# Sixteen more activations kept in SBUF, list making spread over more blocks, and sums paced to the end of a fused transformer layer

## Chip, cores and metric

One core of one Trainium2 chip runs the whole layer as one program. The metric is the device time of one execution in microseconds (us).

## What is computed

One decoder layer over 512 positions of width 1024: attention of two kinds, a norm, and then a retrieval feed-forward (PEER) with 16384 experts, a second norm. The change lies in the feed-forward:

```python
q = (hx @ w_pq).reshape(PEER_CHUNK, PEER_HEADS, 2, PEER_HALF)
sc = jnp.einsum('thpd,hpnd->thpn', q, sub_keys).astype(jnp.float32)
v_half, i_half = lax.top_k(sc, PEER_TOPK)
...
top_s, top_pos = lax.top_k(cand, PEER_TOPK)
idx = jnp.take_along_axis(cand_idx, top_pos, axis=-1)
g = jax.nn.softmax(top_s, axis=-1)
a = jax.nn.gelu(jnp.einsum('thkd,td->thk', u_tab[idx], hx), approximate=False)
return jnp.einsum('thk,thkd->td', (g * a).astype(hx.dtype), v_tab[idx])
```

Each position picks 128 experts (8 heads of 16), takes the dot of its row with each expert's row of `u_tab`, applies gelu, weighs with the gate `g`, and sums the experts' rows of `v_tab`.

## The kernel before

The 512 positions are four tiles of 128. They are served in two ways.

**Dense way**, for the second half of tile 1 and for tiles 2 and 3 (320 positions, `TU`): all 16384 experts are multiplied, in 128 blocks of 128 experts. The first loop ("U blocks", U0 to U127, lines 826 to 836) loads a block of `u_tab` (`raw`, SP queue), splits it into a rounded part `hi` (ScalarE, line 86) and the rest `lo` (VectorE, line 87), and `u_block` (line 802) multiplies it with the normed input `h2h`, `h2l` by 24 matmuls of 320 columns into `st`; ScalarE applies gelu (line 812). The result of U0 to U31 (`a_r`) stays in SBUF; that of U32 to U127 (`a_s`, `NS` = 96) is written to DRAM (`a_d`, line 817, ScalarE's DMA queue) and read again later (`a_b`, line 871, SP queue).

The second loop ("V blocks", V0 to V127 in the order of `order`, lines 893 to 938) multiplies the activation of a block with its gate (`w`, lines 874 and 875), splits that (`wh`, `wl`), loads and splits a block of `v_tab`, and accumulates by 18 matmuls of 512 columns (`v_mm`, three tiles, two halves). The gate of eight blocks (1.5 MB) is loaded at a time by `g_load` (line 851, ScalarE's DMA queue) into `gl`, one group ahead, from `g_d` in DRAM. The last six V blocks (`LAST`) are multiplied at the end, tile by tile and half by half, each half followed by its norm (`finish`).

**Sparse way**, for tile 0 and the first half of tile 1: the chosen rows are fetched by indirect DMA on GpSimd's queue (`fetch`, line 741, 128 rows of 4 KB each, five buffers `gb`), and VectorE takes a dot (line 746) or adds the weighted row (a "sum", line 782). The half tile needs 64 fetches of `u_tab` (its other half of the lists shares the partitions), and its result goes into the gate of tile 1; tile 0 needs 128 fetches of `u_tab` and 128 of `v_tab`.

Beside the U blocks two more things are made: the **lists** of the four tiles (`topk`, VectorE mostly, in the order 1, 2, 3, 0) and the **gate** of tiles 2, 3, 1 (`make_g`: 16 steps for each tile on VectorE, ScalarE and TensorE, 8 stores of 1 MB to `g_d`, line 699). These, the dots and the sums are Python generators whose steps yield a cost; `pull` runs steps until a budget per block is used up: 2.6 for lists until list 1 is there, 1.6 after; `GRATE` = 0.52 gate steps per block once list 2 is there; `RA` = 1.7 for the half tile's dots and `RB` = 1.9 for tile 0's (a dot costs 1.25); in the V loop 1.6 per block (a sum costs 1.2), and at V116 all that is left (`pull(gt, 1e9)`, line 917), followed by tile 0's norm. Tile 0's dots begin when the half tile is done and list 0 is there (`gather_tile`); the gate of tile 1 begins when the half tile is done. `paced` keeps each dot and sum on VectorE behind the split of the block before the last.

Within these ties a scheduler, when the program is built, gives each engine its fixed order of instructions, by program order and by its planned times. Pools share SBUF as a stack: `gl`, `a_b`, `w`, `wh`, `wl` of the V stage (`vp`) lie where the lists and the gate's tiles (`sel`, `gp`) were; `h2h` and `h2l` lie in the pool `hpool` under the tags `hh` and `hl`, which `hi4` and `lo4`, the splits of V124 to V127, take over at the end.

Of the kernel before, what the change touches and what calls it, by code (L numbers as in the profile page):

```python
# [11 lines left out]
F32 = mybir.dt.float32  # L12
# [8 lines left out]
P = 128  # L21
# [6 lines left out]
NKEY = 128  # L28
DT = NT - 1
TD = DT * P  # L30
TG = 16
NTG = TD // TG
# [3 lines left out]
LOWEST = -3.0e38  # L36
NB = 32
GB = 8
NS = 96
GRATE = 0.52  # L40
HU = 64
T0U = P + HU
TU = S - T0U
LAST = 6
GBUF = 5
RA = 1.7
RB = 1.9


@with_exitstack  # L50
def layer(ctx: ExitStack, tc: tile.TileContext, A, out, dbg=None):
# [6 lines left out]
    hpool = ctx.enter_context(tc.tile_pool(name="hpool", bufs=1))  # L58
# [12 lines left out]
    g2_d = dram.tile([1, D], F32, name="g2_d")  # L71
    a_d = [dram.tile([P, TU], F32, name=f"a_d{e}") for e in range(NS)]
    g_d = dram.tile([NTG, P, NKEY, TG], F32, name="g_d")
# [21 lines left out]
    def mm3(ps, lh, ll, rh, rl, first, last):  # L95
        nc.tensor.matmul(ps, lh, rh, start=first, stop=False)  # L96
        nc.tensor.matmul(ps, lh, rl, start=False, stop=False)  # L97
        nc.tensor.matmul(ps, ll, rh, start=False, stop=last)  # L98
# [18 lines left out]
    hh = hpool.tile([P, KB, S], F32R, name="hh", tag="hh")  # L117
# [57 lines left out]
    def drain(g, n=None):  # L175
        i = 0
        while n is None or i < n:
            try:
                next(g)
            except StopIteration:  # L180
                return False
            i += 1
        return True
# [361 lines left out]
    sel_stack = ExitStack()  # L545
# [29 lines left out]
    def u_split(e):  # L575
        return split(load_raw(A["u_T"][e], [P, KB, P]), [P, KB, P])
# [23 lines left out]
    ring = ring_stack.enter_context(tc.tile_pool(name="ring", bufs=1, side="right", reuse_waits="tile"))  # L600
# [101 lines left out]
    best = {}  # L702
    budget = [0.0]
# [4 lines left out]
    weighted = []  # L708
# [19 lines left out]
    def all_g(pool, tk):  # L728
        for t in (2, 3):
            while t not in best:  # L730
                budget[0] -= next(tk, 0.0)
            yield from make_g(t, pool)
        while not weighted:
            yield
        yield from make_g(1, pool)
# [55 lines left out]
    def pull(gen, us):  # L791
        while us > 0:
            try:
                cost = next(gen)
            except StopIteration:
                return us
            if cost is None:
                return 0.0
            us -= cost
        return us  # L800

    def u_block(e):
        hi, lo = early.pop(e) if e in early else u_split(e)
        ps = psq[0].tile([P, TU], F32, name="st", tag="st", bufs=psq[1])
        for k in range(KB):
            mm3(ps, hi[:, k, :], lo[:, k, :], h2h[:, k, T0U:], h2l[:, k, T0U:], k == 0, k == KB - 1)
        pace[0], pace_next[0] = pace_next[0], split.last
        if NB <= e < NB + NS:
            a = ring.tile([P, TU], F32, name="a_s", tag="a_s", bufs=3)
        else:  # L810
            a = ring.tile([P, TU], F32, name="a_r", tag="a_r", bufs=NB)
        nc.scalar.activation(a, ps, AF.Gelu)
        acts[e] = a

    def keep(e):
        if NB <= e < NB + NS:
            nc.scalar.dma_start(a_d[e - NB], acts[e])
            acts[e] = None

    g_stack = ExitStack()  # L820
    gp = g_stack.enter_context(tc.tile_pool(name="gp", bufs=1, reuse_waits="tile"))
    tk = all_topk(gp)
    gg = all_g(gp, tk)
    c1 = c2 = 0.0
    gt = gathers()
    for e in range(NB + NS):
        u_block(e)
        keep(e)
        budget[0] = pull(tk, budget[0] + (2.6 if 1 not in best else 1.6))
        if 2 in best:  # L830
            c1 += GRATE
            while c1 >= 1.0:
                c1 -= 1.0
                drain(gg, 1)
        if 1 in lists:
            c2 = pull(gt, c2 + (RA if not weighted else RB))
    pull(tk, 1e9)
    while not weighted:
        next(gt)
    drain(gg)  # L840
    g_stack.close()
    sel_stack.close()
    psB_stack.close()
    psq[:] = ctx.enter_context(tc.tile_pool(name="psC", bufs=1, space=bass.MemoryType.PSUM, reuse_waits="tile")), 2, 6

# [1 line left out]
    vp = v_stack.enter_context(tc.tile_pool(name="vp", bufs=1, reuse_waits="tile"))  # L847
    pacc = [[accbank() for _ in range(2)] for _ in range(DT)]
    order = list(range(NB)) + list(range(NB + NS, NKEY)) + list(range(NB, NB + NS))

    def g_load(e):
        gl = vp.tile([P, NTG, GB * TG], F32, name="gl", tag="gl", bufs=2)
        nc.scalar.dma_start(gl, g_d.rearrange("g p i t -> p g (i t)")[:, :, e * TG:(e + GB) * TG])
        return gl

# [34 lines left out]
    c2 = 0.0  # L890
    tail = [None]
    last = []
    for n in range(NKEY):
        if n % GB == 0 and n + GB < NKEY:
            gls[order[n + GB]] = g_load(order[n + GB])
        if n + NB + NS < NKEY:
            u_block(n + NB + NS)
            c2 = pull(gt, c2 + 3.6)
        else:
            c2 = pull(gt, c2 + 1.6)  # L900
        if n == NKEY - 16:
            ring_stack.close()
            fin = ctx.enter_context(tc.tile_pool(name="fin", bufs=1, side="right", reuse_waits="tile"))
            tail[0] = fin
            g2r, ln2g, ln2b = (fin.tile([P, D], F32, name=nm) for nm in ("g2r", "ln2g", "ln2b"))
            dma(g2r, g2_d[0].partition_broadcast(P))
            dma(ln2g, A["ln2_g"].partition_broadcast(P))
            dma(ln2b, A["ln2_b"].partition_broadcast(P))
            xr = [fin.tile([P, D], F32, name=f"xr{t}") for t in range(NT)]
            for t in range(NT):  # L910
                dma(xr[t], x1_d[t])
            pre = [h2n] + [fin.tile([P, D], F32, name=f"pre{t}") for t in range(DT)]
            hi4 = hpool.tile([P, 4, D], F32R, name="hi4", tag="hh")
            lo4 = hpool.tile([P, 4, D], F32R, name="lo4", tag="hl")
            tail += [hi4, lo4]
        if n == NKEY - 12:
            pull(gt, 1e9)

            def finish(t, src):
                def half(s, f):  # L920
                    nc.vector.tensor_mul(pre[t][:, s], src[f], g2r[:, s])
                    nc.vector.scalar_tensor_tensor(pre[t][:, s], xr[t][:, s], ALPHA, pre[t][:, s],
                                                   op0=OP.mult, op1=OP.add)

                normalize(vp, pre[t], half)
                for f in range(2):
                    fs = slice(f * 512, (f + 1) * 512)
                    nc.vector.tensor_mul(pre[t][:, fs], pre[t][:, fs], ln2g[:, fs])
                    nc.vector.tensor_add(pre[t][:, fs], pre[t][:, fs], ln2b[:, fs])
                    dma(out[t][:, fs], pre[t][:, fs])  # L930

            finish(0, (acc0[:, 0:512], acc0[:, 512:1024]))
        blk = v_block(n)
        if n < NKEY - LAST:
            for t in range(DT):
                v_mm(t, *blk)
        else:
            last.append(blk)
# [79 lines left out]
```

## Time and profile before

| | us |
|---|---|
| median of 3 runs | 1553.13 (1549.42 to 1555.18) |
| the profiled execution | 1551.68 |
| its span, first to last instruction | 1549.9 |

| engine | busy us | share of the span |
|---|---|---|
| TensorE (PE) | 1432.2 | 92% |
| VectorE (DVE) | 1267.8 | 82% |
| ScalarE (ACT) | 826.1 | 53% |
| GpSimd (POOL) | 466.8 | 30% |

The attention and the scores take the first 362 us, the U blocks run to 981, the V blocks to 1536.6. All times in rows are us from the start of the span; the profile names lines of the kernel above (L741 is line 741). A tile's name in a row stands left of `<-` for what is written and right of it for what is read; buffer numbers are left out. PEclk is the granted clock of TensorE as a part of 2.4 GHz. The DMA share is the mean busy share of the 16 DMA engines.

### The profile page before, as it was taken

What the parts mean: (1) busy time and instruction counts of PE and PEld (TensorE: products, weight loads), DVE (VectorE), ACT (ScalarE), POOL (GpSimd) and SP (SyncE); (2) the same over time, 40 slices, a digit from 0 to 9 for tenths busy, and PEclk for the clock granted to TensorE, in tenths of its full rate; (3) what the DMA queues carried; (4) which work ended last, traced back from release to release, by engine and by line L of the source; (5) the groups of instructions that cost most, each with busy time, mean ns of one, the idle gap of its engine ahead of it and who ended that gap; (6) DMA issues with size and microseconds to landing.
All of it is one profiled execution on the core that took longest, in us unless ns stands there. A gap on an engine that the chain in (4) does not pass through costs nothing.

```text
span 1549.9 us, 22874 instructions
## 1 busy us (share of the span) xinstructions
PE 1432.2 (92%) x7837; PEld 1254.3 (81%) x7837; DVE 1267.8 (82%) x2606; ACT 826.1 (53%) x1523; POOL 466.8 (30%) x338
## 2 busy tenths in 40 slices
PE   6999998998688899999999969999989999989996
PEld 5777776888687889999999969888868778868884
DVE  7897676999888998798879848989778788879766
ACT  2465534334357889899799834344333343334440
POOL 0000000000433334454544525545434443532000
PEclk9999998999999999999999989999989999999998
DMA  8856363222767789999999999999999999999751
GB/s 312 289 182 200 130 212 103 83 85 92 250 239 283 238 310 375 357 408 394 416 342 390 405 362 409 382 379 346 340 385 342 368 372 355 363 337 362 233 171 48
DMA packets 184855, 451.43 MB, mean 291 GB/s; under 512 B 15841, under 2 KB 90977, under 8 KB 181538
## 3 DMA queue, kind: packets, MB, share of 16 engines
q1 hardware_dynamic: 75426, 241.28, 43.0%
q0 software_dynamic: 46080, 167.79, 28.9%
q10 hardware_dynamic: 63232, 40.90, 8.7%
q8 instruction: 61, 1.00, 0.3%
q14 instruction: 56, 0.46, 0.1%
HBM read 404.00 MB, written 45.88 MB: 290 GB/s over the span
## 4 chain that ended last, share of the span: by engine, by line
PE 47%; issue 14%; DMA 13%; DVE 11%; POOL 8%; ACT 5%; POOLq 0%; SPq 0%; DVEq 0%; ACTq 0%
POOL gb L741 8%; PE acc L97 7%; PE acc L98 7%; PE acc L96 7%; DMA raw<-v_blk 5%; PE bank L96 5%; PE bank L97 4%; PE bank L98 4%; DMA gl<-g_d 3%; DMA raw<-u_T 3%; DVE lo L87 3%; PE st L96 2%; PE st L98 2%; PE st L97 2%; ACT hi L86 2%
## 5 line engine op out<-in xcount | busy, mean ns | idle before, releaser
L86 ACT CAST hi<-raw 128x1024 fp32r<-128x1024 f32 x286 | 299.8, 1050 | 333.5 <-DMA raw<-v_blk 111.4
L87 DVE TENSOR_TENSOR lo<-raw,hi 128x1024 fp32r<-128x1024 f32 x286 | 348.7, 1221 | 119.0 <-ACT hi L86 113.4
L96 PE MATMUL st<-h2h,hi 128*128 128x320 f32 x1024 | 326.3, 319 | 27.6 <-ACT hi L86 27.6
L98 PE MATMUL st<-h2h,lo 128*128 128x320 f32 x1024 | 322.0, 316 | 17.5 <-DVE lo L87 17.5
L97 PE MATMUL st<-h2l,hi 128*128 128x320 f32 x1024 | 321.7, 314 | 0.0
L96 PE MATMUL acc<-hi,wh 128*128 128x512 f32 x768 | 302.2, 394 | 17.3 <-ACT hi L86 17.0
L97 PE MATMUL acc<-lo,wh 128*128 128x512 f32 x768 | 303.8, 396 | 5.0 <-DVE lo L87 4.6
L98 PE MATMUL acc<-hi,wl 128*128 128x512 f32 x768 | 301.8, 393 | 0.0
L741 POOL DMA_INDIRECT gb<-v_tab,ei x128 | 182.4, 1425 | 240.2 <-DVE acc L782 222.3
L746 DVE SCALAR_TENSOR_TENSOR gb<-gb,h2n 128x1024 f32<-128x1024 f32 x192 | 230.7, 1218 | 21.2 <-DMA gb<-u_tab,ei 15.4
L741 POOL DMA_INDIRECT gb<-u_tab,ei x128 | 183.4, 1433 | 196.5 <-DVE gb L746 182.1
L96 PEld LDWEIGHTS st<-h2h,hi 128*128 128x128 f32 x1024 | 196.5, 192 | 31.2 <-ACT hi L86 31.2
L98 PEld LDWEIGHTS st<-h2h,lo 128*128 128x128 f32 x1024 | 196.0, 192 | 20.5 <-DVE lo L87 20.5
L97 PEld LDWEIGHTS st<-h2l,hi 128*128 128x128 f32 x1024 | 196.3, 192 | 0.0
L96 PEld LDWEIGHTS acc<-hi,wh 128*128 128x128 f32 x768 | 145.9, 190 | 49.8 <-ACT hi L86 18.7
L97 PEld LDWEIGHTS acc<-lo,wh 128*128 128x128 f32 x768 | 145.8, 190 | 41.7 <-DVE lo L87 10.4
L688 ACT ACTIVATE go<-oh,iT 128x128 f32<-128x128 bf16 x384 | 169.7, 525 | 9.4 <-DVE oh L682 7.5
L741 POOL DMA_INDIRECT gb<-u_tab,eip x64 | 91.0, 1422 | 272.1 <-ACT hi L86 148.7
L98 PEld LDWEIGHTS acc<-hi,wl 128*128 128x128 f32 x768 | 145.9, 190 | 30.3
L782 DVE SCALAR_TENSOR_TENSOR acc<-gb,w,acc 128x1024 f32<-128x1024 f32 x127 | 162.2, 1277 | 0.0
L104 POOL TENSOR_TENSOR rs_r<-rs_v,mhalf 128x1 f32<-128x1 f32 (+1 forms) x12 | 9.3, 775 | 364.1 <-DVE rs_v L102 328.3
L692 PE MATMUL acc<-go,oh 128*128 128x128 f32 x768 | 108.5, 284 | 7.3 <-ACT go L688 7.1
(213 smaller groups left out, 1988.9 us busy)
## 6 DMA issues: line engine op xcount, KB each, us to landing
raw<-u_T SPq DMA_DIRECT2D x128, 512.0 KB
raw<-v_blk SPq DMA_DIRECT2D x128, 512.0 KB
wada<-w_adaT SPq DMA_DIRECT2D x48, 512.0 KB
g_d<-stage SPq DMA_DIRECT2D x24, 1024.0 KB
gl<-g_d ACTq DMA_DIRECT2D x16, 1536.0 KB
a_d<-a_s ACTq DMA_DIRECT2D x96, 160.0 KB
a_b<-a_d SPq DMA_DIRECT2D x96, 160.0 KB
raw<-w_pqT SPq DMA_DIRECT2D x16, 512.0 KB
```

The lines of the kernel that those rows point to most:

```text
L86: nc.scalar.copy(hi, src)
L87: split.last = nc.vector.tensor_sub(lo, src, hi.bitcast(F32))
L96: nc.tensor.matmul(ps, lh, rh, start=first, stop=False)
L97: nc.tensor.matmul(ps, lh, rl, start=False, stop=False)
L98: nc.tensor.matmul(ps, ll, rh, start=False, stop=last)
L104: nc.gpsimd.tensor_tensor(r, v, mhalf.to_broadcast([P, n]), op=OP.pow)
L688: nc.scalar.activation(go[:, i, :], oh0[:, :, i], AF.Copy, scale=iT[:, 2, t0 + i:t0 + i + 1])
L692: nc.tensor.matmul(ps[:, i * P:(i + 1) * P], oh1[:, 4 * u + i, :], go[:, 4 * u + i, :], start=True, stop=True)
L741: nc.gpsimd.indirect_dma_start(out=b, out_offset=None, in_=A[tab], in_offset=bass.IndirectOffsetOnAxis(ap=idx[:, j:j + 1], axis=0))
L746: paced(nc.vector.scalar_tensor_tensor(b, b, 1.0, h2n, op0=OP.mult, op1=OP.mult, accum_out=acc))
L782: paced(nc.vector.scalar_tensor_tensor(acc0, b, w0[:, j:j + 1], acc0, op0=OP.mult, op1=OP.add))
```

## The change

The number of activations that go through DRAM falls from 96 to 80. Before U112 the loop now finishes the lists, the half tile and the gate, closes their pools, and opens a pool `late` of 16 tiles in their place, where the activations of U112 to U127 stay; the V loop takes these after the first 32. One of the two `gl` buffers moves to the place of `h2h` (tag `hh`). The lists' budget falls from 1.6 to 0.7 per block once list 2 is there. The half tile's dots get 1.6 instead of 1.7 per block, the gate 0.54 steps instead of 0.52, tile 0's sums 1.45 per V block instead of 1.6. (The branches for U blocks inside the V loop were not reached before either, since 32 + 96 = 128.)

```diff
-NS = 96
-GRATE = 0.52
+NS = 80
+GRATE = 0.54
...
-RA = 1.7
+RA = 1.6
 RB = 1.9
+RV = 1.45
...
         if NB <= e < NB + NS:
             a = ring.tile([P, TU], F32, name="a_s", tag="a_s", bufs=3)
+        elif e < NB:
+            a = ring.tile([P, TU], F32, name="a_r", tag="a_r", bufs=NB)
         else:
-            a = ring.tile([P, TU], F32, name="a_r", tag="a_r", bufs=NB)
+            a = late[0].tile([P, TU], F32, name="a_l", tag="a_l", bufs=NKEY - NB - NS)
...
-    for e in range(NB + NS):
+    late = []
+    for e in range(NKEY):
+        if e == NB + NS:
+            pull(tk, 1e9)
+            while not weighted:
+                next(gt)
+            drain(gg)
+            g_stack.close()
+            sel_stack.close()
+            late.append(ctx.enter_context(tc.tile_pool(name="late", bufs=1, reuse_waits="tile")))
         u_block(e)
         keep(e)
-        budget[0] = pull(tk, budget[0] + (2.6 if 1 not in best else 1.6))
-        if 2 in best:
+        if e < NB + NS:
+            budget[0] = pull(tk, budget[0] + (2.6 if 1 not in best else 1.6 if 2 not in best else 0.7))
+        if 2 in best and e < NB + NS:
...
-    pull(tk, 1e9)
-    while not weighted:
-        next(gt)
-    drain(gg)
-    g_stack.close()
-    sel_stack.close()
...
     def g_load(e):
-        gl = vp.tile([P, NTG, GB * TG], F32, name="gl", tag="gl", bufs=2)
+        if e // GB % 2 == 0:
+            gl = vp.tile([P, NTG, GB * TG], F32, name="gl", tag="gl", bufs=1)
+        else:
+            gl = hpool.tile([P, NTG, GB * TG], F32, name="gl2", tag="hh")
...
-        if n + NB + NS < NKEY:
-            u_block(n + NB + NS)
-            c2 = pull(gt, c2 + 3.6)
-        else:
-            c2 = pull(gt, c2 + 1.6)
+        c2 = pull(gt, c2 + RV)
```

## Rows read from the trace of the kernel before

**Rows 1.** The page's totals: busy us, share of the span, instructions.

```profile
PE 1432.2 (92%) x7837; PEld 1254.3 (81%) x7837; DVE 1267.8 (82%) x2606; ACT 826.1 (53%) x1523; POOL 466.8 (30%) x338
```

**Rows 2.** Stages: length, busy per engine (PE, PEld, DVE, ACT, POOL), PEclk, DMA share, GB/s.

```profile
440.00:640.00 200.00, 181.22 (x1198) 171.40 (x1198) 173.91 (x379) 161.78 (x273) 75.34 (x52) 0.98 0.82 298
...
907.00:932.00 25.00, 10.82 (x55) 10.16 (x54) 7.37 (x11) 4.02 (x6) 4.01 (x3) 0.66 1.00 326
...
981.00:1095.00 114.00, 112.76 (x496) 92.42 (x495) 104.42 (x137) 46.50 (x85) 56.53 (x40) 1.00 1.01 362
1095.00:1415.00 320.00, 299.45 (x1272) 242.67 (x1271) 256.09 (x305) 119.51 (x212) 132.81 (x94) 0.96 1.00 359
1415.00:1500.00 85.00, 85.00 (x376) 70.38 (x375) 59.42 (x85) 34.77 (x64) 1.98 (x2) 1.00 0.75 241
```

**Rows 3.** Timeline of TensorE, like matmuls of two U blocks: start, duration, instruction.

```profile
939.79 0.31 PE L97 MATMUL st<-h2l,hi 128*128 128x320 f32 x1
...
943.31 0.31 PE L97 MATMUL st<-h2l,hi 128*128 128x320 f32 x1
```

**Rows 4.** Timeline of TensorE, like matmuls of two V blocks.

```profile
1484.15 0.39 PE L98 MATMUL acc<-hi,wl 128*128 128x512 f32 x1
...
1488.23 0.39 PE L98 MATMUL acc<-hi,wl 128*128 128x512 f32 x1
```

**Rows 5.** Stages, `st` alone: length, busy PE, PEld, ACT, PEclk, DMA share, GB/s.

```profile
440.00:565.00 125.00, 88.07 (x536) 80.97 (x537) 9.61 (x22) 0.97 0.72 252
565.00:640.00 75.00, 60.22 (x372) 54.66 (x370) 6.54 (x15) 1.00 0.98 374
640.00:880.00 240.00, 196.39 (x1279) 187.65 (x1277) 23.01 (x53) 1.00 1.00 386
932.00:981.00 49.00, 46.52 (x317) 46.26 (x315) 5.79 (x14) 1.00 1.03 413
```

**Rows 6.** Timeline of ScalarE and TensorE, 913 to 924; in brackets the wait and its releaser.

```profile
913.58 0.77 ACT L812 ACTIVATE a_s<-st 128x320 f32<-128x320 f32 x2 [10.49 <-DMA g_d<-stage]
914.05 8.16 ACTq L817 DMA_DIRECT2D a_d<-a_s  x2
...
923.41 0.64 PE L96 MATMUL st<-h2h,hi 128*128 128x320 f32 x1 [11.52 <-ACT hi L86]
```

**Rows 7.** Timeline of the end: the last cast of `v_blk`, the last matmul.

```profile
1513.36 1.05 ACT L866 CAST hi<-raw 128x1024 fp32r<-128x1024 f32 x1 [1.24 <-DMA raw<-v_blk]
...
1536.19 0.39 PE L98 MATMUL acc<-hi,wl 128*128 128x512 f32 x1
```

**Rows 8.** The chain that ended last, and TensorE's timeline, near 1100.

```profile
1095.04 27.57 DMA gl<-g_d
...
1130.77 0.80 PE L96 MATMUL acc<-hi,wh 128*128 128x512 f32 x1 [7.33 <-ACT hi L86]
```

**Rows 9.** Waits of the SP queue, 1000 to 1420: total us, times, longest.

```profile
SPq L871 <- DMA gl<-g_d: 52.9, 5, 14.5
```

**Rows 10.** Timeline of ScalarE's queue: the third `gl` load.

```profile
997.49 0.38 ACTq L853 DMA_DIRECT2D gl<-g_d  x1
```

**Rows 11.** The page's DMA issues: queue, count, size of one.

```profile
raw<-v_blk SPq DMA_DIRECT2D x128, 512.0 KB
...
gl<-g_d ACTq DMA_DIRECT2D x16, 1536.0 KB
...
a_b<-a_d SPq DMA_DIRECT2D x96, 160.0 KB
```

**Rows 12.** Groups by line and form on VectorE: busy us, mean ns, idle before.

```profile
L87 DVE TENSOR_TENSOR lo<-raw,hi 128x1024 fp32r<-128x1024 f32 x286 | 348.7, 1221 | 119.0 <-ACT hi L86 113.4 <-issue 2.2 <-ACT stage L695 1.4
...
L782 DVE SCALAR_TENSOR_TENSOR acc<-gb,w,acc 128x1024 f32<-128x1024 f32 x127 | 162.2, 1277 | 0.0
...
L881 DVE TENSOR_TENSOR wl<-w,wh 128x384 fp32r<-128x384 f32 x128 | 69.7, 551 | 26.7 <-ACT wh L880 26.7
...
L875 DVE TENSOR_TENSOR w<-a_b,gl 128x320 f32<-128x320 f32 x96 | 46.5, 485 | 2.9 <-DMA a_b<-a_d 2.4
```

## What the change was predicted to do

> **What bounds the kernel now.** I read the totals first: TensorE is busy 92% of the span, VectorE 82% [rows 1]. The change touches no matmul, so the question is where TensorE waits. The table by stage answers it [rows 2]. U and V blocks are numbered U0 to U127 and V0 to V127 in the order of the program; a U block has 24 matmuls, a V block 18. Their own pace is the distance of like matmuls: 24 apart in U 3.52 us (939.79 to 943.31) [rows 3], 18 apart in V 4.08 us (1484.15 to 1488.23) [rows 4].
>
> Three stretches lose time against these paces.
> - U blocks by matmuls of `st` [rows 5]: 440 to 565, 536/24 = 22.3 blocks, 5.60 us each; 565 to 640, 15.5 blocks, 4.84 each; 640 to 880, 53.3 blocks, 4.50 each (the gate's own matmuls lie between, so 3.52 is not reachable there). In 440 to 565 the last two lists are made on VectorE at full rate, beside the half tile's dots; there the DMA is not the bound (252 GB/s), afterwards it is full (386).
> - 907 to 932: 55 matmuls are 8 us of work, 17 us are lost, and the granted clock is 0.66, part of it at 1.2 GHz [rows 2]. The rows of ScalarE tell why: it stands 10.49 us in front of the first `gl` load until the last `g_d` has landed, then its next `a_d` issue is held 8.16 us; TensorE waits 11.52 us for `hi` [rows 6].
> - V: 981 to 1536.6 (last matmul 1536.19 [rows 7]) is 555.5 us for 128 x 4.08 = 522, a loss of 33. Nearly all is in 1095 to 1415: 1272/18 = 70.7 blocks in 320 us, 4.53 each, at a DMA share of 1.00 and 359 GB/s; from 1415, when the sums' fetches are over, no loss and DMA at 0.75 [rows 2]. One chain of it is shown [rows 8]: a `gl` load takes 27.57 us, the SP queue goes on only behind it, and TensorE then waits 7.33 us for `hi`. For `a_b` alone SP waits 52.9 us on `gl` loads in 1000 to 1420 [rows 9].
>
> **The change part by part.** The kernel's own costs give the order: per block a pull adds a budget, each step takes its cost off. Counted so, before: list 1 ready in U6, list 2 U17, 3 U27, 0 U38; half tile done U53, 114 of the 128 dots of tile 0 done at U127, sums from V10 to V106. After: 1 U6, 2 U17, 3 U40, 0 U65; half tile done U55; ten blocks without a fetch, since tile 0's dots need list 0; 96 dots done at U127, sums from V27; at 1.45 per block 109 sums are done when V116 pulls the rest, so 19 come at once.
>
> *Lists 3 and 0 spread (0.7 instead of 1.6 per block).* U17 to U55 take 21 x 5.60 + 17 x 4.84 = 199.9 us now. A block with 1.6 of list work costs 0.76 us over one without [rows 5]. If that scales, 0.7 costs 0.33: 38 x 5.17 = 196.5. If VectorE then has room, TensorE and DMA hold the pace of 640 to 880: 38 x 4.50 = 171. I take 4.95, nearer to the first since VectorE still is busy 174 of 200 us in 440 to 640 [rows 2]: 188, a gain of 12 (3 to 29). Blocks U55 to U65 lose their fetches, but stay at TensorE's 4.50: 0. Fewer dots at 1.6 instead of 1.7 in U6 to U17: 1 us.
>
> *No `a_d` for U112 to U127.* In 932 to 981 a block takes 49/13.2 = 3.71 us at 413 GB/s [rows 5]; without 0.16 MB per block the demand is 0.524 + 1.52 x 0.524 = 1.32 MB in 3.52 us, 375 GB/s, below that: 16 x 0.19 = 3 us (0 to 3). The activations' new pool lies where the list and gate tiles were; their last reader is the gate of U105, seven blocks earlier, so the added wait of the gelus on ScalarE (behind it: casts `hi`, in turn all of U) is already over: 0.
>
> *The stall at 907 to 932.* `gl` must still wait for the last `g_d` on ScalarE's queue, now after U105 instead of U109. Same price: 0. If no `a_d` follows the load, 8 us go; if `late` tiles wait too, 8 come.
>
> *Every second `gl` in the buffer of `h2h`.* Its first load, now beside U blocks, cannot start before U's last matmul. It would be issued some 33 us ahead of V8, or 16 ahead of V8's `w`, which VectorE makes four blocks early (the third load takes the buffer that V0 to V7 read, and was issued at 997.49, four blocks after 981 [rows 10]). At 26 to 28 us a load VectorE waits some 7 us, with `lo`, sums and fetches queued behind it; TensorE has buffered blocks: 2 us (0 to 7). At the end `hi4` wants the same buffer while the last group's `gl` is still read by V120 to V127, so the casts of V124 to V127 come after V127's `w`, and the last `raw` load after the first of them: 3 us (0 to 5). This path ended the V stage before (last cast 1513.36 [rows 7]).
>
> *16 reads of `a_b` fewer, sums at 1.21 instead of 1.33 per block.* A V block moves 0.524 (`raw`) + 0.197 (an eighth of `gl`) MB, 0.164 of `a_b` if its activation was stored [rows 11], and 0.524 (128 rows of 4 KB) per sum. Before, from V32: 1.584 MB, 388 GB/s at 4.08 us, against 359 measured: this is the loss. After, up to V48: 1.354 MB, 332 GB/s: no loss by bandwidth; the cluster of `xr` loads behind `gl` near V31 stays, 5 us (0 to 9) of about 9. From V48 to the end: 80 x 0.524 + 76 x 0.164 + 9 x 1.573 + 101.5 x 0.524 = 121.8 MB. At 359 GB/s 339 us, and from the landing of the last `raw` to TensorE's end 23.2 (its cast 1513.36, end 1536.6 [rows 7]): 362, counted from TensorE at V45, three buffers behind. TensorE alone needs 83 x 4.08 = 338.6. Loss 24 (12 at 371 GB/s, 33 at 350). It falls late: the last 19 sums are 19 x 1.277 = 24 us of VectorE [rows 12] and 10 MB ahead of V116 to V127.
>
> V after: 1.6 + 2 + 5 + 24 + 3 = 36 lost, against 33: +3. U: -12 - 1 - 3 = -16. Sum -13 on the profiled 1551.7 (span 1549.9 and 1.8 around it): 1538.7. That run lies 1.4 below the median of the three: I say 1540.
>
> The rule that speaks against my bound: in U the same queues move 413 GB/s, in V 359 [rows 2, 5]; I take 359, since V's mix has the `gl` and `a_b` rows. The Trainium skill (HBM Reference, Specifications) says that a core streaming alone gets about 425 GB/s; by it V48 to the end would be an estimated 287 us and V not bound by DMA at all. No stretch of V here shows that rate.
>
> **The rivals.**
> - *DMA lets go of V.* If the lighter mix moves at U's 413 GB/s, V48 to the end is 295 us and TensorE's 338.6 rules; what is left is VectorE's tail: from the burst 24 + 12 x (1.221 + 0.485 + 0.551) = 51 [rows 12] and some 8 for tile 0's norm, 59 us, against 41 until TensorE wants V127: 18. V loses 1.6 + 5 + 18 = 25, -8; U -16: 1528; down to 1510 where the lists also reach the pace of 4.50. For it: 413 in U. Against: all of 1095 to 1415 at share 1.00.
> - *The burst holds the end (slower).* The order puts all 19 sums and the norm before V116. Then these fetches, 10 MB, and the blocks' own loads must land before VectorE goes on: some 54 us at 359 GB/s where TensorE has buffers for 12, and `hi4` on top. The tail then costs 33 instead of 10, `gl` 7: V loses 60, +27. It decides from the point where this exceeds what U gains; with U at -10: 1569. For it: last six blocks are multiplied by halves, so the last `lo` is wanted 21 us before the end. Against: SP and POOL load side by side.
> - *It does not do what it says.* The scheduler orders each engine by its own planned times, so the lists may bunch as before and the fetches end no later: U -6, V +5: 1551.
>
> **How the numbers follow.** Forecast (1527 to 1550) 0.40, DMA lets go 0.22, no effect 0.20, burst 0.18. About 0.5%, 8 us, is what a measurement of this kernel can tell from no change. Of the forecast 0.34 is faster by more than that: faster 0.56; same 0.06 + 0.19 = 0.25; slower 0.18 + 0.01 = 0.19. Range 1515 to 1565: it leaves out the upper part of the burst and the lowest of the second case, under 0.2 together.
>
> **What would show it.** Right: blocks between the second list and the half tile's end at about 4.95 us; a stretch of some 45 us without POOL fetches; the 1.2 GHz stall of ScalarE before `gl` still there; V at full pace until its 48th block; fetches that end some 12 blocks later, with TensorE waiting for `hi` or `lo` in the last 15. Wrong: U as slow as before with the lists spread (then ScalarE's gate work held it), V stalls that begin before V48, or DMA above 380 GB/s in V.

## The result and the profile after

The changed kernel takes 1546.93 us (median; 1535.94 to 1559.32) against 1555.18 us of the kernel before (1549.19 to 1561.81): ratio 0.9944, 95% interval 0.9927 to 0.9962. The ratio leaves out the execution of 1559.32 us, which counts as a slow one. That is 8.2 us by the medians and 0.56% by the ratio; 1540 was predicted, with 1515 to 1565 as range.

The profiled execution spans 1545.7 us, against 1549.9. I cut both at two points, the start of the last matmul of `st` (end of U) and the end of the span. U from its first `st` matmul that reads `lo`: 618.0 us before (360.2 to 978.2), 603.2 after (365.6 to 968.8), so 14.8 less. From there to the end: 571.7 before, 576.9 after, so 5.2 more. The remaining 5.4 us are U's later start, in front of anything that the change touches; this start lies between 360 and 367 us in all the kernels below, so I compare lengths, not times.

The totals hardly differ from [rows 1]:

```profile
PE 1430.1 (93%) x7837; PEld 1254.9 (81%) x7837; DVE 1265.8 (82%) x2606; ACT 822.6 (53%) x1523; POOL 462.5 (30%) x338
```

**U.** The `st` matmuls alone by stage (length, busy PE, PEld, ACT, PEclk, DMA share, GB/s), answering [rows 5]:

```profile
440.00:565.00 125.00, 97.25 (x631) 93.09 (x631) 11.31 (x26) 0.99 0.88 312
565.00:640.00 75.00, 54.54 (x350) 51.39 (x349) 6.48 (x15) 0.95 0.86 298
640.00:880.00 240.00, 193.01 (x1253) 184.06 (x1252) 22.13 (x51) 1.00 0.95 361
932.00:968.00 36.00, 36.00 (x248) 36.00 (x247) 4.28 (x10) 1.00 1.00 390
```

631 matmuls in 440 to 565 are 26.3 blocks of 4.75 us, where they were 22.3 of 5.60. In 565 to 640 a block takes 5.14 instead of 4.84, in 640 to 880 4.60 instead of 4.50, and at the end of U 36/10.3 = 3.48. Before, that pace was the same: the last line of [rows 5] runs to 981, but U's last matmul starts at 978.2, and up to there a block takes 46.2/13.2 = 3.51, not 3.71.

```profile
932.00:978.20 46.20, 46.20 (x316) 46.20 (x315) 5.60 (x13) 1.00 1.03 413
```

Windows cut at fixed times mix blocks, so I also count by blocks (every 24th `st` matmul is a new one). U17 to U55, which the prediction named as the blocks beside the last two lists, take 202.0 us before and 189.8 after (38 blocks are 912 matmuls, the edges add one or two; busy PE, PEclk, DMA share, GB/s):

```profile
447.40:649.40 202.00, 149.57 (x913) 0.98 0.82 298
```

```profile
448.40:638.20 189.80, 141.84 (x914) 0.97 0.87 307
```

That is 12.2 us less. U0 to U17 take 4.4 less (but 82.8 to 88.2 us in all the kernels below, so much of that can be scatter), U55 to U109 take 4.3 more, U109 to the end 2.4 less.

GpSimd's queue has a hole, as its longest wait shows (in 560 to 700; total, times, longest): it stands until the fourth list (`ei`) is ready.

```profile
POOL gb L742 <- DVE ei L717: 53.6, 1, 53.6
```

The stall of [rows 6] is still there, earlier, since the gate ends four blocks sooner (ScalarE's and TensorE's timeline):

```profile
890.54 0.43 ACTq L863 DMA_DIRECT2D gl<-g_d  x1
891.06 0.77 ACT L815 ACTIVATE a_s<-st 128x320 f32<-128x320 f32 x2 [8.69 <-DMA g_d<-stage]
891.53 7.87 ACTq L820 DMA_DIRECT2D a_d<-a_s  x2
...
899.49 1.04 ACT L87 CAST hi<-raw 128x1024 fp32r<-128x1024 f32 x1 [7.66 <-issue]
...
900.59 0.63 PE L97 MATMUL st<-h2h,hi 128*128 128x320 f32 x1 [11.61 <-ACT hi L87]
```

**V.** TensorE's `acc` matmuls by stretch (length, busy, PEclk, DMA share, GB/s), first before, then after. 18 matmuls at full pace are 4.08 us [rows 4]; what a stretch has beyond that is lost.

```profile
978.20:1095.00 116.80, 115.39 (x506) 1.00 1.01 363
1095.00:1160.00 65.00, 57.21 (x240) 0.92 1.00 367
1160.00:1440.00 280.00, 267.25 (x1144) 0.98 1.00 354
1440.00:1537.00 97.00, 96.16 (x419) 1.00 0.52 161
```

```profile
960.00:1095.00 135.00, 121.19 (x522) 0.97 0.97 337
1095.00:1160.00 65.00, 54.14 (x224) 0.89 0.89 310
1160.00:1440.00 280.00, 280.00 (x1236) 1.00 1.02 366
1440.00:1537.00 97.00, 79.97 (x328) 0.92 0.65 241
```

Lost before: 2.1, 10.6, 20.7 and, up to the end of the last matmul at 1536.6, 1.6 us: 35. Lost after, from 968.8 and up to 1527.0: 7.9, 14.2, 0 and 12.7: 35 again. The middle is free, the first and the last stretch pay for it.

The first loss is the second `gl` list, which can start only when U no longer reads `h2h` (ScalarE's and TensorE's timeline):

```profile
971.31 0.38 ACTq L863 DMA_DIRECT2D gl<-g_d  x1
...
996.71 0.25 ACT L884 COPY w<-gl 128x64 f32<-128x64 f32 x1 [10.75 <-DMA gl<-g_d]
...
998.30 0.79 PE L97 MATMUL acc<-hi,wh 128*128 128x512 f32 x1 [4.24 <-ACT hi L87]
```

The second stands where [rows 8] showed one: the seven loads for the last norms (`xr` and three more, 0.5 MB each) go out from 1086 to 1118 us, beside a `gl` load. A step of the chain of waits, SP's wait for it with a `raw` load in hand (in 1090 to 1170), TensorE's wait behind that.

```profile
1087.38 30.15 DMA gl<-g_d
...
SPq L93 <- DMA gl<-g_d: 22.0, 1, 22.0
...
1126.65 0.79 PE L97 MATMUL acc<-hi,wh 128*128 128x512 f32 x1 [9.38 <-ACT hi L87]
```

The last is VectorE's. All engines in 1440 to 1500 (VectorE is the third pair), then the last cast and the last matmul, answering [rows 7]:

```profile
1440.00:1500.00 60.00, 53.09 (x224) 41.25 (x223) 57.88 (x69) 20.18 (x34) 26.68 (x22) 0.99 0.92 344
...
1512.68 1.05 ACT L876 CAST hi<-raw 128x1024 fp32r<-128x1024 f32 x1 [2.59 <-DMA raw<-v_blk]
...
1526.63 0.39 PE L99 MATMUL acc<-hi,wl 128*128 128x512 f32 x1
```

VectorE is busy 57.88 of 60 us; 25 sums stand in that stretch, where before there was none after 1428. The last cast comes 0.7 us earlier than before, although U ended 9.4 us earlier.

### The profile page after: what moved, and what is told of

Same layout as the page of the kernel before. It is cut to its first block, busy times and chain, and to the rows that moved or that the text cites. A ratio compares the mean times of both kernels' runs of the same rounds, so it can differ in the third digit from the quotient of the medians.

```text
span 1545.7 us, 22766 instructions
## 1 busy us (share of the span) xinstructions
PE 1430.1 (93%) x7837; PEld 1254.9 (81%) x7837; DVE 1265.8 (82%) x2606; ACT 822.6 (53%) x1523; POOL 462.5 (30%) x338
## 4 chain that ended last, share of the span: by engine, by line
PE 49%; DVE 15%; issue 11%; DMA 9%; ACT 9%; POOL 5%; POOLq 0%; DVEq 0%; ACTq 0%; SPq 0%
PE acc L97 9%; PE acc L98 9%; PE acc L99 8%; POOL gb L742 5%; PE bank L97 5%; PE bank L98 4%; PE bank L99 4%; ACT go L689 4%; DMA gl<-g_d 4%; DVE lo L88 3%; DMA raw<-v_blk 2%; ACT hi L87 2%; PE st L98 2%; PE st L97 2%; PE st L99 2%
## 5 line engine op out<-in xcount | busy, mean ns | idle before, releaser
L99 PE MATMUL st<-h2h,lo 128*128 128x320 f32 x1024 | 319.7, 313 | 15.9 <-DVE lo L88 15.7
L742 POOL DMA_INDIRECT gb<-u_tab,ei x128 | 179.4, 1402 | 261.2 <-DVE gb L747 192.4
L97 PEld LDWEIGHTS st<-h2h,hi 128*128 128x128 f32 x1024 | 194.9, 190 | 22.3 <-ACT hi L87 22.2
L890 ACT CAST wh<-w 128x384 fp32r<-128x384 f32 x128 | 64.7, 511 | 117.1 <-PE acc L98 70.9
## 6 DMA issues: line engine op xcount, KB each, us to landing
gl<-g_d ACTq DMA_DIRECT2D x16, 1536.0 KB, 16.5
```

Source lines behind the costliest of these rows:

```text
L742: nc.gpsimd.indirect_dma_start(out=b, out_offset=None, in_=A[tab], in_offset=bass.IndirectOffsetOnAxis(ap=idx[:, j:j + 1], axis=0))
L890: nc.scalar.copy(wh, w)
```

## The experiments

All were timed beside the kernel before, and each ratio is to it (e1 to e4 on one chip, e5 to e8 on a second, f1 to f4 on a third). "U" and "V to end" are the two lengths of one profiled execution as cut above; "dots in V" are dots of tile 0 left when U ends, "late sums" those that start after 1440 us.

| kernel | ratio (95%) | U | V to end | dots in V | late sums |
|---|---|---|---|---|---|
| before | 1 | 618.0 | 571.7 | 12 | 0 |
| the change | 0.9944 (0.9927 to 0.9962) | 603.2 | 576.9 | 28 | 25 |
| e1 lists alone | 0.9949 (0.9922 to 0.9976) | 605.2 | 579.6 | 30 | 14 |
| e2 activations alone | 1.0025 (0.9992 to 1.0059) | 614.3 | 578.7 | 11 | 0 |
| e3 sums 1.7 | 0.9965 (0.9934 to 0.9995) | 601.1 | 582.2 | 28 | 4 |
| e4 sums 1.3 | 0.9924 (0.9894 to 0.9954) | 604.3 | 571.1 | 28 | 28 |
| e5 lists, sums 1.3 | 0.9997 (0.9964 to 1.0029) | 602.5 | 583.5 | 30 | 34 |
| e6 first `gl` on GpSimd | 0.9894 (0.9862 to 0.9926) | 598.0 | 573.4 | 28 | 23 |
| e7 `hi4` apart | 0.9975 (0.9946 to 1.0003) | 602.1 | 577.9 | 28 | 25 |
| e8 no burst | 0.9959 (0.9926 to 0.9991) | 598.4 | 586.3 | 28 | 25 |
| f1 second `gl` apart | 0.9954 (0.9925 to 0.9983) | 602.5 | 576.1 | 29 | 24 |
| f2 loads held | 0.9943 (0.9913 to 0.9974) | 602.0 | 585.8 | 28 | 21 |
| f3 e4 and e6 | 0.9915 (0.9883 to 0.9947) | 595.0 | 571.5 | 28 | 28 |
| f4 f3, lists at 0.9 | 0.9830 (0.9783 to 0.9876) | 598.5 | 555.0 | 15 | 14 |

The two lengths come from one execution each. The change, e3, e4, e7, e8, f1 and f2 differ in nothing before U112, and their U takes 598.4 to 604.3 us: a difference of up to 6 us between two lengths can be scatter.

My first theory: the spread lists are the gain, the kept activations relieve the DMA in V, and the burst of 19 sums (those that V116 pulls at once) takes part of it back. The rival: the slower sums relieve V, whatever is kept.

### e1: the lists alone, on the kernel before

```
-  budget[0] = pull(tk, budget[0] + (2.6 if 1 not in best else 1.6))
+  budget[0] = pull(tk, budget[0] + (2.6 if 1 not in best else 1.6 if 2 not in best else 0.7))
```

> The kernel before with the lists' budget alone changed (0.7 per block once list 2 is there). Own theory: the U blocks end some 12 us earlier (969 instead of 981), V keeps its loss of 33 us and gets a burst of 8 sums at V116, some 4 us: 8 us faster than before, ratio 0.995. Rival, the lists pay nothing in the end: tile 0's fetches start ten blocks later, and V, full of DMA, gives all of it back: ratio 1.000 with a U stage that ends early and a V loss of 45.

One number of one line gives 0.9949, as its theory said and as much as the whole change (the intervals overlap). U is as short as the change's within the scatter: U17 to U55 take 189.8 us here too, and 187 to 193 in every kernel with the slower lists, against 202.4 in e2, which has the old rate. V keeps its waits (5.78 us at 1117, 2.71 at 1272, 3.09 at 1306, 4.22 at 1379) and gets longer, since 30 dots are now left for it instead of 12.

### e2: the kept activations and the shared buffer alone, with the old rates

```
-            budget[0] = pull(tk, budget[0] + (2.6 if 1 not in best else 1.6 if 2 not in best else 0.7))
+            budget[0] = pull(tk, budget[0] + (2.6 if 1 not in best else 1.6))
-GRATE = 0.54
+GRATE = 0.52
-RA = 1.6
+RA = 1.7
-RV = 1.45
+RV = 1.6
```

> The change without its rates: 16 activations on chip, gl's second buffer in the place of h2h, but lists 1.6, gate 0.52, half tile 1.7 and sums 1.6 as before. Own theory, the fewer reads relieve V: U ends at 978, V waits for its first gl2 (4 us) and near V31 as before, and has little loss after V48: V loss 33 down to 20, 15 us faster than before, ratio 0.990. Rival, it is the slower sums (1.21 per block) that took V's DMA below its limit, not the reads: at 1.33 sums V still loses some 30, ratio 0.997.

1.0025: my theory falls here. With 1.33 sums a block V stalls as before (3.47 us at 1137, 4.07 at 1246, 5.08 at 1391), though 16 reads are gone, and the second `gl` costs 7.32 us at 1009. Together with the shared buffer, and without the new rates, the kept activations gain nothing.

### e3 and e4: the change with faster and with slower sums

```
-RV = 1.45
+RV = 1.7
```

> The changed kernel with 1.7 instead of 1.45 per V block for tile 0's dots and sums: no sums are left for V116. Own theory, the last 12 us of V's loss come from the 19 sums at V116 and the DMA has room left between V48 and V116: 8 to 10 us faster than the changed kernel, ratio to before 0.989. Rival, DMA bounds that stretch: 1.63 MB per block at 365 GB/s is 4.47 us instead of 4.08, 26 us more over 68 blocks, against 12 gained at the end: ratio 1.003.

```
-RV = 1.45
+RV = 1.3
```

> The changed kernel with 1.3 per V block: 37 instead of 19 sums are left for V116. Own theory, the order puts them on VectorE before the last blocks' work: 18 x 1.28 = 23 us more of VectorE there, 18 to 22 us slower than the changed kernel, ratio to before 1.007. Rival, sums and blocks share the time and the end is set elsewhere (by hi4's wait or the last loads): within 5 us of the changed kernel, ratio 0.995 to 0.998.

Both go against my theory, and neither ratio lies where a rival had it (e3: 0.9965, where 0.989 or 1.003 was expected; e4: 0.9924, where 1.007 or 0.995 to 0.998 was). TensorE's `acc` in 1160 to 1440 of e3, and of e4:

```profile
1160.00:1440.00 280.00, 263.07 (x1115) 0.97 1.01 361
```

```profile
1160.00:1440.00 280.00, 280.00 (x1237) 1.00 1.01 357
1440.00:1537.00 97.00, 60.28 (x236) 0.84 0.62 233
```

The arithmetic of the prediction fits this stretch. At 1.7/1.2 = 1.42 sums a block needs 0.524 + 0.197 + 0.164 + 1.42 x 0.524 = 1.63 MB, which at the measured 361 GB/s takes 4.51 us; 62 blocks x 0.43 = 27 us. Measured: 280 - 1115/18 x 4.08 = 27.3. At 1.3 a block needs 1.45 MB, 356 GB/s at full pace: no loss. At 1.45 it needs 372 and got 366. So the rate of the sums frees the middle of V. The price is a burst of 37 sums in e4. TensorE then waits for `hi4`:

```profile
1497.38 1.65 PE L97 MATMUL acc<-hi,wh 128*128 128x512 f32 x3 [9.99 <-ACT hi L876]
```

V to end is still 571.1 against 576.9. But the intervals of the two ratios overlap: that 1.3 is better than 1.45 as a whole is not shown.

### e5: are the two rates all of it?

```
-        budget[0] = pull(tk, budget[0] + (2.6 if 1 not in best else 1.6))
+        budget[0] = pull(tk, budget[0] + (2.6 if 1 not in best else 1.6 if 2 not in best else 0.7))
-            c2 = pull(gt, c2 + 1.6)
+            c2 = pull(gt, c2 + 1.3)
```

> The kernel before with the slow list rate of the change and with sums at 1.3 a block instead of 1.6, and nothing else: 96 activations still go out and come back, both buffers of the gates' lists are free. After the first four runs my theory is that the two rates are all of the gain and that the 16 kept activations are worth nothing, since their buffer arrangement starts the second list of gates 7 us late (4.24 to 7.32 us of PE wait for it in the runs with it). Theory: ratio 0.989 to 0.992 (the kernel before with only the list rate had 0.995, and the slower sums gave another 0.002 to 0.004 where the change's own sums were slowed from 1.45 to 1.3). Rival: the slower sums pay only because 16 reads fewer leave the DMA room in the second loop; then this run stays at 0.994 to 0.995 and waits of 2 to 5 us stand between 1160 and 1440 us as in the run with the list rate alone.

Neither number came: 0.9997, so e1's gain is not seen here, though the two intervals overlap (0.9964 to 0.9976). Its `acc` by stretch:

```profile
960.00:1095.00 135.00, 121.42 (x527) 0.99 0.94 328
1095.00:1160.00 65.00, 62.57 (x267) 0.97 0.99 355
1160.00:1440.00 280.00, 277.86 (x1212) 0.99 1.02 356
1440.00:1537.00 97.00, 73.14 (x302) 0.97 0.74 276
```

From the end of U (969.6) to 1440 it loses 5.9 + 4.5 + 5.3 = 15.7 us, where e4 loses 3, and then 34 sums are late instead of 28. So my second theory fell too. With slow sums the change's arrangement is worth 0.7% (the intervals of e4 and e5, timed on two chips, don't meet), with fast sums (e2) nothing. e4 and e5 also differ in the rates of the gate and of the dots (GRATE, RA) and in 2 dots, and I have no run that separates these from the 16 reads: that part stays open.

### e6: the first `gl` load on GpSimd's queue

```
-        nc.scalar.dma_start(gl, g_d.rearrange("g p i t -> p g (i t)")[:, :, e * TG:(e + GB) * TG])
+        (nc.gpsimd if e == order[0] else nc.scalar).dma_start(gl, g_d.rearrange("g p i t -> p g (i t)")[:, :, e * TG:(e + GB) * TG])
```

> The change with one edit: the load of the first eight gates is issued on GpSimd's queue, not on ScalarE's. In the trace of the change ScalarE stands 8.69 us before 891.06 (waiting with that load for the last store of gates) and then 7.66 us in the issue of two stores of activations right behind it, and TensorE loses 11.61 + 2.65 us at 900 to 904. Theory: the place in ScalarE's queue makes the wait, so 10 to 14 us go: ratio 0.986 to 0.989. Rival 1: the loop over u is short of data there in any case (a wait of 3.62 us for raw stands ahead of it), the wait only changes its name: 0.993 to 0.995. Rival 2: GpSimd's queue now holds the rows for the dots behind the same wait, VectorE stands in a dot and the splits behind it wait: 0.995 to 1.000.

0.9894, at the edge of what the theory gave and clear of both rivals. TensorE's `st` in 880 to 915 of the change, then of e6, and e6's longest wait there:

```profile
880.00:915.00 35.00, 20.74 (x127) 0.80 0.92 322
```

```profile
880.00:915.00 35.00, 28.68 (x179) 0.90 1.03 395
...
909.68 0.64 PE L97 MATMUL st<-h2h,hi 128*128 128x320 f32 x1 [5.96 <-ACT hi L87]
```

52 more matmuls are 52/24 x 3.52 = 7.6 us. What made most of the stall was the place of one DMA in ScalarE's queue. What is left, 5.96 us, waits for the same ScalarE: it now stands 10.26 us before 908.01 with `w` in front of the landing `gl`. The Trainium skill (DMA: Bandwidth & Descriptors, Issuing engines are not separate DMA queues) says that starting DMAs from several engines saves only the time on the sequencer that it takes to initiate them, usually small beside the DMA itself. Here ScalarE had stood 8.69 us in front of the issue and 7.66 us in the next two issues: the latter is such time and was not small, and the former, a wait for a store, is not what that sentence speaks of.

### e7 and e8: two cures for the end

e7 gives `hi4` a buffer of its own, in the space of the kept activations, so that it doesn't wait for the last `gl`:

```
-            late.append(ctx.enter_context(tc.tile_pool(name="late", bufs=1, reuse_waits="tile")))
+            late_stack = ExitStack()
+            late.append(late_stack.enter_context(tc.tile_pool(name="late", bufs=1, side="right", reuse_waits="tile")))
...
+            late_stack.close()
             ring_stack.close()
...
-            hi4 = hpool.tile([P, 4, D], F32R, name="hi4", tag="hh")
+            hi4 = fin.tile([P, 4, D], F32R, name="hi4")
```

> The change with the first parts of the last four blocks (hi4) in a buffer of their own, in the space of the kept activations, instead of the space in which the last eight gates lie. In the trace of the change these casts run three in a row after the last w (1506.7 us on). Theory: that wait is a small part of the end; the sums and the norm of the first tile hold VectorE there: 2 to 4 us less, ratio 0.992 to 0.993. Rival 1: nothing, the end is VectorE's work alone: 0.994 to 0.995. Rival 2: the wait is most of the end's loss (it was 9.99 us in the run with sums at 1.3): 0.988 to 0.990.

e8 takes the burst and the norm of tile 0 out of the block loop and puts them behind it:

```
         if n == NKEY - 12:
-            pull(gt, 1e9)
...
-            finish(0, (acc0[:, 0:512], acc0[:, 512:1024]))
...
             last.append(blk)
+    pull(gt, 1e9)
+    finish(0, (acc0[:, 0:512], acc0[:, 512:1024]))
```

> The change without the burst: sums go on at 1.45 a block to the last block, and the last few with the norm of the first tile come after the loop over v, where TensorE still has the last six blocks' matmuls (24.5 us) to run. Theory: the burst of 19 sums (24 us of VectorE) and the norm of the first tile (about 10 us) in twelve blocks are what costs 9 to 12 us between 1415 and 1526; without them the last matmul comes 8 to 10 us earlier and the norm of the first tile has its place beside the last matmuls: 5 to 9 us less, ratio 0.988 to 0.991. Rival: the work only moves behind the last splits, the norm of the second tile waits for it and the end comes no earlier: 0.993 to 0.997.

Neither gains (0.9975 and 0.9959; the intervals overlap the change's). In e7 V to end is 577.9 against 576.9. Between 1440 us and its last matmul TensorE waits 6.9 us for `wh`, which waits for VectorE's `w`, as it does 5.8 us in the change: VectorE sets the pace there whether or not the casts must wait. But e7 changed one thing more. With `late` on the right side the last norms' loads lie in its place too, so they go out from 1152 instead of 1086, and the wait behind them comes later:

```profile
1186.22 0.79 PE L97 MATMUL acc<-hi,wh 128*128 128x512 f32 x1 [5.19 <-ACT hi L87]
```

So e7 does not measure the price of `hi4` alone. In e8 the last matmul comes at 1523.2, then 25.2 us follow, where the change has 19.1 and the kernel before 13.7: tile 0's norm (about 7.6 us of VectorE) now stands among the other three. The work only moved, as the rival said.

### f1 and f2: take away the two waits at the beginning of V

f1 gives the second `gl` list its own buffer again and keeps the 16 activations:

```
-        if e // GB % 2 == 0:
-            gl = vp.tile([P, NTG, GB * TG], F32, name="gl", tag="gl", bufs=1)
-        else:
-            gl = hpool.tile([P, NTG, GB * TG], F32, name="gl2", tag="hh")
+        gl = vp.tile([P, NTG, GB * TG], F32, name="gl", tag="gl", bufs=2)
...
-            a = vp.tile([P, TU], F32, name="a_b", tag="a_b", bufs=4)
+            a = vp.tile([P, TU], F32, name="a_b", tag="a_b", bufs=3)
```

(and `late` on the right side, as in e7, so that the last norms' loads go out from 1145 here too)

> The change with a second buffer of its own for the lists of gates (as before), bought with three instead of four buffers for the activations read back and with the kept activations placed so that the last tiles' inputs can reuse them; 16 activations are still kept. In the change the second list can start only when the loop over u has ended (971.31 us) and TensorE waits 4.24 us for it at 998 (4.47, 5.53 and 6.63 us in three runs since). Theory: that wait is the price of the shared place, so 4 to 7 us go: ratio 0.990 to 0.992. Rival: the second loop lacks data at its start whatever the order, an earlier second list (1.5 MB) only takes it from the rows of v and of the table then, and the wait comes back under another name at 1100 to 1130: 0.994 to 0.997.

f2 holds the last norms' loads back to V112:

```
+            xr = [fin.tile([P, D], F32, name=f"xr{t}") for t in range(NT)]
+            for b in [g2r, ln2g, ln2b] + xr:
+                paced(nc.vector.memset(b[:, 0:1], 0.0))
             dma(g2r, g2_d[0].partition_broadcast(P))
...
-            xr = [fin.tile([P, D], F32, name=f"xr{t}") for t in range(NT)]
```

> The change with the seven loads for the last norms (0.5 MB each, 3.7 MB, 10 us at 360 GB/s) held back to the block for which they are written (the 112th of the second loop) by a one-column write of each tile on VectorE. In the change they are issued from 1086 to 1118 us, in SyncE's queue between the rows of v, and TensorE waits 9.38 us at 1126. Theory: that crowd of loads makes the wait at 1126, which goes, and the end has room for them, since VectorE sets its pace there: 6 to 9 us less, ratio 0.988 to 0.990. Rival 1: the wait at 1126 comes from sums that run ahead of the DMA there (it was absent when sums came at 1.3 a block, with these loads in place): it stays, 0.994 to 0.995. Rival 2: the loads at the end hold up the rows of v there and give the gain back: 0.993 to 0.998 without a wait at 1126.

The waits at 998 (f1) and at 1126 (f2) went, and both times are the change's: 0.9954 and 0.9943. `acc` of f1 up to 1440 with its longest wait, then of f2 from 1160 with its own:

```profile
960.00:1095.00 135.00, 124.74 (x548) 1.00 0.99 345
1095.00:1160.00 65.00, 65.00 (x288) 1.00 0.96 333
1160.00:1440.00 280.00, 266.43 (x1145) 0.98 0.99 352
...
1179.95 0.80 PE L97 MATMUL acc<-hi,wh 128*128 128x512 f32 x1 [4.96 <-ACT hi L87]
```

```profile
1160.00:1440.00 280.00, 276.33 (x1207) 0.99 1.01 359
1440.00:1537.00 97.00, 70.99 (x285) 0.90 0.65 235
...
1463.42 0.80 PE L97 MATMUL acc<-hi,wh 128*128 128x512 f32 x1 [12.00 <-ACT hi L87]
```

f1 loses 1.7 us before 1095 instead of 7.9 and nothing in 1095 to 1160, and then 20.5 in 1160 to 1440, where the change loses none. f2 loses nothing at 1126 and 12.00 at one place at 1463, where its loads now crowd. The rivals had both ratios right; f1's had the lost time come back at 1100 to 1130, and it came later. f1 isn't a clean test: its activations have three buffers instead of four and its loads moved, and e7, where the loads moved too, loses 17.1 in 1160 to 1440 (f1: 20.5).

The wait of the crowd goes where the seven loads go (1126 in the change, 1186 in e7, 1180 in f1, 1463 in f2). But the loads alone don't make it. In e4, which differs from the change in the rate of the sums alone, they go out from 1079 to 1104, and TensorE's `acc` there loses 2.0 us instead of 14.2:

```profile
1095.00:1160.00 65.00, 63.56 (x278) 1.00 1.00 349
```

### f3 and f4: the two gains together, and more dots in U

f3 is e4 and e6 together. f4 is f3 with

```
-            budget[0] = pull(tk, budget[0] + (2.6 if 1 not in best else 1.6 if 2 not in best else 0.7))
+            budget[0] = pull(tk, budget[0] + (2.6 if 1 not in best else 1.6 if 2 not in best else 0.9))
```

> The change with two edits that gained by themselves: the first list of gates issued on GpSimd's queue (0.9894) and sums at 1.3 a block (0.9924). Theory: they act in different stages (900 us; 1100 to 1440 us) and add up: 0.986 to 0.989. Rival: the burst of 37 sums that is left keeps VectorE as the bound of the last blocks, which end no earlier because the loop over u ended earlier: 0.990 to 0.993.

> As the run with both edits, and the lists of the third and fourth tile at 0.9 a block instead of 0.7. At 0.7 the fourth list is ready some ten blocks after the half tile's dots are done, and GpSimd's queue has nothing to fetch for 53.6 us (640 to 680 us); at 0.9 it is ready about when they end, so some 12 more dots are done in the loop over u and as many fewer sums are left for the burst (about 20 of 37). Theory: VectorE's time at the end falls by 12 to 16 us, of which the end shows half: 0.981 to 0.985. Rival: the lists at 0.9 cost TensorE in the loop over u (the blocks beside lists at 1.6 took 5.60 us against 4.50) what the end gains: 0.986 to 0.990.

f3 takes 1535.00 us. Whether the two gains add up stays open: the ratio, 0.9915, is the rival's, but its interval (0.9883 to 0.9947) holds a part of what the theory gave, the two medians (1553.58 before) give 0.988, and the profiled lengths do add up. U and V to end together are 13.6 us below the change's, where e4 is 4.7 and e6 8.7 below. At the end 28 sums are late, and TensorE stands 10.22 us at 1493 for `hi4`. f4 takes 1523.22 us, 0.983, within what its theory gave, and beats both kernels. Its wait of GpSimd for the fourth list (560 to 700), all engines in 640 to 880, and `acc` in V:

```profile
POOL gb L742 <- DVE ei L717: 15.3, 1, 15.3
...
640.00:880.00 240.00, 235.03 (x1686) 232.12 (x1685) 205.13 (x272) 216.60 (x390) 116.38 (x81) 1.00 1.00 386
...
960.00:1095.00 135.00, 129.63 (x568) 1.00 0.98 341
1095.00:1160.00 65.00, 62.58 (x269) 0.97 0.94 322
1160.00:1440.00 280.00, 280.00 (x1237) 1.00 1.01 360
1440.00:1537.00 97.00, 56.02 (x235) 0.93 0.42 158
```

The hole falls from 53.6 to 15.3 us, and 13 more dots are done in U, for 3.5 us of U's length. V to end falls by 16.5 us: 13 rows fewer are 6.8 MB, 19 us at 360 GB/s, or 13 x 1.28 = 16.6 us of VectorE; no run separates the two. Only 14 sums are late, and no TensorE wait over 2.2 us is left after 990 us.

## Why the prediction held, and where its terms were off

*The list term was right in size and in cause.* The blocks from U17 to U55 take 189.8 us, 4.99 each (188 and 4.95 predicted), 12.2 less (12 predicted), and e1 and e2 show that this one rate does it. The hole in GpSimd's fetches is 53.6 us (45), and the stall before `gl` has its old price.

*U's other terms were not right, and its sum, 14.8 against 16, came close partly by luck.* "No `a_d`", 3 us, is worth nothing: its 3.71 came from a stretch that ran past U's end (U's last matmul starts at 978.2, not 981), and U116 to the end of U takes 3.51 a block before and after. U55 to U109 was given no cost and takes 4.3 us more, alike within 0.1 in every kernel that has the change's U rates. In e1, with the gate at 0.52 and the dots at 1.7, it costs 1.6, so most of it comes with what e1 lacks; which part of that is open.

*V's sum was right, its parts were not: that is luck.* Predicted loss 36, measured 35; one part too high by 14 (24 for V48 to the end and 3 for `hi4`, against 12.7) covers two that were too low by 9 and 4.
- V48 to the end was priced at 24 us, at 359 GB/s. Measured is 0 up to 1440 and 12.7 after. The DMA moved 366 GB/s there; the bound of 12 at 371 was the nearer one. The end's loss was priced by the DMA's bytes, and it is mostly VectorE's: busy 57.88 of 60 us while the DMA share falls to 0.92.
- The `xr` cluster, 5 us (0 to 9), measured 14.2 in 1095 to 1160 against 10.6 before. The step that failed was that fewer reads and slower sums would thin it. It needs the seven loads (f2) and sums at 1.45: at 1.3 (e4) the same stretch loses 2.0.
- The second `gl`, 2 us (0 to 7): the stretch to 1095 loses 7.9 instead of 2.1, so 5.8 more, in the upper part of the bound.

*One term was missing.* The sum ended V at TensorE's last matmul. With the sums late, the last splits are late as well, the last matmuls run close behind them, and the three norms bunch up: 19.1 us follow the last matmul, not 13.7 (16 in e6, e7 and f1 with as many late sums, so part of the 19.1 is scatter). With this, V to end is 5.2 us longer where 3 was predicted. -14.8 + 5.2 = -9.6, against -13. The medians say -8.2.

*What the prediction priced right without seeing its weight:* it counted that 18 more dots would be left for V (128 - 96 against 128 - 114; 28 and 12 were left, 16 more), and let them push the sums back, without a price of their own. They bring 16 x 0.524 = 8.4 MB into V, where the kept activations take 16 x 0.164 = 2.6 MB out. The step from f3 to f4 shows that this is what the change gives away; taking out the wait for the shared buffer (f1) or for the crowd of loads (f2) gave no time. The wish to relieve VectorE at 440 to 640 moved rows from U, where the DMA had room (312 GB/s in 440 to 565, a hole of 53.6 us), into V, where it has none.

*The rivals.* "DMA lets go of V" was right for 1160 to 1440, though at 366 GB/s and not 413, and mostly because the sums are slower: that stretch loses 20.5 us in e2 and 27.3 in e3, with faster sums, and 5.3 in e5, with slow sums and all the reads. "The burst holds the end" was right about the place and wrong about the price: a burst of 37 (e4) costs V less than sums at 1.7 a block do (571.1 against 582.2). "It does not do what it says" fell: the blocks beside the lists went from 5.32 to 4.99 us, and the hole came.

## What to carry to other kernels

Where a stage is bound by what the DMA brings, taking away one wait in it can give nothing (f1, f2): count the bytes and the vector work that the stage must get through, and move some of it to an earlier stage that has room (f4: 13 rows moved, 16.5 us gained). Set a spread rate so that the next consumer in the queue is fed just when the one before ends: 0.7 left a hole of 53.6 us, 0.9 one of 15.3. And look at what a DMA issue that must wait does to the compute queue it sits in: moving one such issue was worth as much as the whole change (e6).

## What the runs showed of the hardware that I had not expected

- The rate that V gets depends little on its mix: 354 GB/s before, 357 (e4), 361 (e3), 366 (the change) in 1160 to 1440, always at a DMA share of 1.00 to 1.02. I had taken 359 as a ceiling of that mix; 367 came over 275 us without a wait (the change, 1165 to 1440). The Trainium skill (HBM Reference, Specifications) gives about 425 GB/s for a core that streams alone; no stretch here shows that, the most I found over 45 us is 417 (e1, 857 to 902).
- The same 1.5 MB `gl` load lands in 25.32 us from 971.31 and in 30.15 us from 1087.38. During the latter SP, another queue, stood 22.0 us with a `raw` load until that `gl` had landed. In f2, with no `xr` loads around, SP has no wait for `gl` from 1080 to 1130, but it has others later (up to 13.1 us), and in e4 it stands 16.5 us with a `raw` load, with no TensorE wait over 1.5 us behind that. Why one queue waits for the other's load was not tried. The Trainium skill (DMA: Bandwidth & Descriptors, Queues, rings and completion order) says that a load's completion mark lands on an engine only after that engine's earlier writes, of any queue; that would let a `raw` load end with the `gl` ahead of it, but no run here separates it from a mere lack of bytes.
- The two `a_d` issues behind the first `gl` on ScalarE's queue held ScalarE for 7.87 us together; the others take 0.33 each. With that `gl` on GpSimd's queue (e6) no `a_d` issue between 886 and 912 us takes more than 0.33.
